# Gates of a seven-product set issued one and two jobs later, and the sets' weights asked for at the last low part of the tile they replace

## The chip, the cores and the metric

The kernel runs on one core of one Trainium2 chip. The metric is the device time of one execution in microseconds (us), taken as the median of several executions. A core has five engines that run beside each other: TensorE (PE, with PEld for its weight loads), VectorE (DVE), ScalarE (ACT), GpSimd (POOL), and SyncE (SP), which here only issues transfers (DMA).

## What is computed

One decoder block on 512 tokens of width 1024. The part that matters here is the projection of the normed input `u` by the wide matrix `w_in`, and the gates cut from it:

```python
u = rmsnorm(x, ln1_g[i])
proj = u @ w_in[i]
q, k, v, pool_in, z, xbc, dt_raw, gate_pre = jnp.split(proj, split_idx, axis=-1)
...
gates = jax.nn.sigmoid(gate_pre + b_gate[i]).reshape(b, s, N_BRANCH, D_MODEL)
merged = gates[:, :, 0] * y_a + gates[:, :, 1] * y_b + gates[:, :, 2] * y_c
x = x + merged @ w_o[i]
```

`y_b` is the pooled branch; its gate is the one that the change moves. After this comes a gated feed-forward block and a last norm.

## The kernel before

**Numbers in two parts.** Every matrix product is made from a high and a low part of each operand: `wh` is the weight rounded on ACT to TensorE's fast 32-bit form (`cast`, L186, the copies at L195), `wl` is what is left, a subtraction on DVE (`lows`, L208, at L215). A product is three matmuls, high by high, weight-high by activation-low, weight-low by activation-high, in that order (`mm3`, L228). So PE needs `wh` when a product starts, and `wl` for its last third.

**Jobs.** The work is a list of jobs, each one block of weights and a body of matmuls. Before the body of job n is written down, its `prepare` (L1785) writes the low part of job n+1, the cast of job n+2 and the fetch of job n+3. The cast's two halves are held back in a list, `second`, and written by `flush` within the body. There are two buffers for raw weights, three for `wh`, two for `wl`. A job can have a function `then` (L222), which is called right after its low part. Between jobs stand `Call`s, plain functions run at that place of the list. PE, ACT, DVE and POOL work in the order in which the program is written (L106, L1808), each through its own queue; SP's order is laid out by a scheduler from what a transfer has to wait for.

**Sets of seven.** Four times the kernel computes a 2x2 block product by seven products and not eight. The first of these gives values for attention (`v_pair`, L584); after it come three, set 0, 1 and 2 (`set_of_sevens`, L699; L1569 to 1572), on columns of q, of k and of gates. Set 0 makes gates 2 to 5 of branch 1; set 1 makes q and k alone; set 2 one q, one k, and gates 0 and 1. The seven jobs are called one to seven. In a set's job each product has two column blocks of twelve matmuls, 128 weight columns by 256 tokens (`body`, L760): four high by high, four with the activation's low part, four with the weight's low part, then the same for the second block; after each block `flush`, after both `use`, which reads the result from PSUM. Jobs of the values' seven come before, and the jobs of the three sets are interleaved by the list at L1581: one, five, two, three, six of set 0, one of set 1, seven of set 0, five of set 1, four of set 0, and so on.

**The quarter tiles.** One tile of 128x1024 numbers (a `w3`, from a pool of two) holds two quarters of a set's weights, `W[0]` and `W[1]`, each 128x4x256 numbers. `load` (L706) asks for them on SP. Then they are worked on in place: after the low part of one, `W[0] += W[1]` (DVE, L349) and the other quarters are added to `W[1]` by two accumulating transfers of POOL (L370); after the low parts of three and of six, `W[0]` takes in those jobs' raw weights (L349). Five reads the first sum, seven reads `W[1]`, four reads `W[0]` last. The values' seven use two such tiles of their own; its seven is the last reader of one of them and its four of the other, and these are the buffers that set 0 and set 1 take over. Set 2 takes over that of set 0, whose last reader is four of set 0. The calls that load set 0 and set 1 stand behind the bodies of the values' six and seven (L1578), that of set 2 stands before four of set 0 (L1585).

**Gates.** `gate_sink` (L1211) makes one gate of 128 columns by 512 tokens. A gate on the left side is ready in two halves: `two` adds on DVE (L1222) and takes the sigmoid of the first half on ACT (L1216), `four` takes the sigmoid of the second half from PSUM and multiplies the branch's result `MG` (tiles `yo`) by the gate on DVE (L1219). A gate on the right side: `put` subtracts on DVE (L1230), once with six and once with seven, and after the second time takes the sigmoid of the whole (L1216) and multiplies (L1219). Set 0 has two gates of either side, so its seven writes, on DVE, subtraction, multiplication, subtraction, multiplication, each multiplication behind a sigmoid on ACT.

**Sends.** The values' results `v` are sent by SP to tiles `vr` (L606), four small transfers for each block of tokens; they are read by the attention products at L841, long after the sets.

## Time and profile before

| | |
|---|---|
| Median of the runs | 1034.19 us (3 runs, 1032.52 to 1035.01) |
| The profiled execution: its own time | 1035.22 us |
| Its span, first to last instruction | 1033.4 us |
| Granted TensorE clock, mean | 0.997 |
| PE busy | 1022.2 us, 99% |
| PEld busy | 868.8 us, 84% |
| DVE busy | 698.8 us, 68% |
| ACT busy | 485.1 us, 47% |
| POOL busy | 161.2 us, 16% |
| Instructions | 13679 |
| Read from HBM | 118.48 MB, 117 GB/s over the span |
| The values' sevens start on PE | 206.6 us |
| The three sets run on PE | 235.8 to 311.6 us |

Times in the views are us from the start of the span. In a timeline a row has its start, its length, the engine, the line of the kernel, the operation, what it writes and reads, and how many instructions are merged in it; in square brackets stands how long its engine had been idle before it, and what ended that. Successive matmuls overlap, so the distance between the starts of two rows is the pace, and the length of a row is more than that. In a table by windows each row has the window, its length, the busy time of PE, PEld, DVE, ACT and POOL with their numbers of instructions, then the granted clock (1.00 is full speed), the busy share of the DMA engines and the GB/s that they moved. A row of a list of waits has who waited for whom, the us in total, how often, and the longest. The chain of waits is the work that ended last, followed back from the end, and shown in order of time.

### The profile page before, as it was taken

To read this page: it belongs to the slowest core of one execution; us is meant where nothing else is said; L and a number is where in the kernel's file an instruction comes from. 1 tells how busy PE (TensorE), PEld (TensorE's weight loads), DVE (VectorE), ACT (ScalarE), POOL (GpSimd) and SP (SyncE) were. 2 spreads that over 40 slices of the span, in tenths; PEclk is the share of its full clock that TensorE was granted. 3 is DMA by queue.
4 is the path that set the end of the run, shared out by engine and by line. 5 is a ranking of instruction groups with operands and counts; after the bars stand their busy time and mean duration, and the time that the engine had idled before them with its cause. 6 is when DMAs were issued, how large, how long until landed. Compare 5 with 4: busy or idle time off the path is not lost.

```text
span 1033.4 us, 13679 instructions
## 1 busy us (share of the span) xinstructions
PE 1022.2 (99%) x5420; PEld 868.8 (84%) x5420; DVE 698.8 (68%) x938; ACT 485.1 (47%) x811; POOL 161.2 (16%) x135
## 2 busy tenths in 40 slices
PE   9999999999999999999999999999999999999997
PEld 9998878899998888888888888898888888888885
DVE  5563566776767758766768656766768677666775
ACT  6432554455545564557445324545444443443342
POOL 1770000001100004210152501101111001111120
PEclk9999999999999999999999999999999999999999
DMA  8344312156453234552254525443223324323142
GB/s 289 115 127 139 102 62 75 31 116 170 103 133 123 82 109 116 143 133 68 68 152 147 179 82 203 168 144 121 82 100 124 103 82 162 122 82 123 62 143 82
DMA packets 121919, 123.16 MB, mean 119 GB/s; under 512 B 5603, under 2 KB 104230, under 8 KB 121855
## 3 DMA queue, kind: packets, MB, share of 16 engines
q1 hardware_dynamic: 118543, 119.07, 36.6%
q0 software_dynamic: 2720, 2.36, 1.7%
q8 instruction: 42, 0.69, 0.3%
q10 hardware_dynamic: 592, 0.86, 0.2%
q14 instruction: 22, 0.18, 0.1%
HBM read 118.48 MB, written 2.22 MB: 117 GB/s over the span
## 4 chain that ended last, share of the span: by engine, by line
PE 95%; DVE 2%; ACT 1%; DMA 1%; issue 0%; SPq 0%; ACTq 0%; DVEq 0%
PE pa L234 32%; PE pu L234 22%; PE p L234 14%; PE pb L234 8%; PE pqk L234 6%; PE pa L1696 2%; PE ps L800 1%; PE pu L1482 1%; PE ppw L234 1%; PE pt L828 1%; PE po L841 1%; PE py L1126 1%; DVE wl L215 1%; PE pa L1653 1%; DMA w<-in_w_in_dram 1%; PE pyo L1133 1%
## 5 line engine op out<-in xcount | busy, mean ns | idle before, releaser
L215 DVE TENSOR_TENSOR wl<-raw,wh 128x2048 fp32r<-128x2048 f32 (+3 forms) x94 | 208.7, 2222 | 44.9 <-ACT wh L195 35.6
L195 ACT CAST wh<-raw 128x1024 fp32r<-128x1024 f32 (+3 forms) x186 | 180.5, 994 | 46.8 <-DVE raw L339 26.3
L1343 DVE SCALAR_TENSOR_TENSOR hc<-pu,fcol,hc 128x510 f32<-128x510 f32 x88 | 65.8, 748 | 60.9 <-ACT hc L1340 59.3
L234 PE MATMUL pa<-uh,wh 128*128 128x512 f32 x336 | 86.5, 399 | 0.0
L234 PE MATMUL pu<-uh,wl 128*128 128x512 f32 (+1 forms) x352 | 83.7, 380 | 0.0
L234 PE MATMUL pu<-uh,wh 128*128 128x512 f32 (+1 forms) x352 | 83.5, 379 | 0.0
L234 PE MATMUL pu<-ul,wh 128*128 128x512 f32 (+1 forms) x352 | 83.5, 379 | 0.0
L234 PE MATMUL pa<-ul,wh 128*128 128x512 f32 x336 | 83.0, 389 | 0.0
L234 PE MATMUL pa<-uh,wl 128*128 128x512 f32 x336 | 83.0, 389 | 0.0
L234 PEld LDWEIGHTS pu<-uh,wl 128*128 128x128 f32 x352 | 64.1, 188 | 12.8 <-DVE wl L215 0.3
L234 PEld LDWEIGHTS pu<-ul,wh 128*128 128x128 f32 x352 | 64.2, 188 | 12.5
L234 PEld LDWEIGHTS pu<-uh,wh 128*128 128x128 f32 x352 | 64.1, 188 | 12.4
L234 PEld LDWEIGHTS pa<-ul,wh 128*128 128x128 f32 x336 | 63.1, 188 | 13.3
L234 PEld LDWEIGHTS pa<-uh,wl 128*128 128x128 f32 x336 | 63.1, 188 | 13.1
L1348 POOL TENSOR_TENSOR hc<-hc 128x512 f32<-128x512 f32 x22 | 30.4, 1383 | 278.9 <-DVE hc L1343 243.9
L234 PEld LDWEIGHTS pa<-uh,wh 128*128 128x128 f32 x336 | 61.2, 188 | 12.8 <-issue 0.7
L1340 ACT ACTIVATE hc<-pu,fcol,fcol 128x512 f32<-128x512 f32 x40 | 31.2, 779 | 80.3 <-PE pu L234 80.1
L195 ACT CAST wh<-w 128x512 fp32r<-128x512 f32 (+2 forms) x50 | 35.3, 748 | 21.6 <-DVE w L349 10.2
L821 ACT ACTIVATE sb<-sb,both 128x128 f32<-128x128 f32 (+1 forms) x72 | 30.0, 418 | 31.8 <-DVE both L818 21.7
L370 POOL DMA_DIRECT2D w<-in_w_in_dram x10 | 12.3, 1229 | 203.8 <-DVE w L349 150.8
L215 DVE TENSOR_TENSOR wl<-w,wh 128x1024 fp32r<-128x1024 f32 (+2 forms) x25 | 38.4, 1540 | 8.1 <-ACT wh L195 5.9
L1345 ACT ACTIVATE hc<-hc 128x512 f32<-128x512 f32 x22 | 13.9, 632 | 42.7 <-DVE hc L1343 42.7
(381 smaller groups left out, 1950.1 us busy)
## 6 DMA issues: line engine op xcount, KB each, us to landing
raw<-in_ffn_w_up_dram SPq DMA_DIRECT2D x22, 1024.0 KB
raw<-in_w_in_dram SPq DMA_DIRECT2D x21, 1024.0 KB
raw<-in_ffn_w_down_dram SPq DMA_DIRECT2D x11, 1024.0 KB
raw<-in_w_in_dram SPq DMA_DIRECT2D x20, 512.0 KB
raw<-in_w_o_dram SPq DMA_DIRECT2D x8, 1024.0 KB
raw<-in_w_b_dram SPq DMA_DIRECT2D x4, 1024.0 KB
al<-ad SPq DMA_DIRECT2D x16, 256.0 KB
w<-in_ffn_w_down_dram SPq DMA_DIRECT2D x4, 1024.0 KB
```

The lines of the kernel that those rows point to most:

```text
L195: act.copy(job.high[:, :, o], job.raw[:, :, o])
L215: (eng or dve).tensor_tensor(l[:, :, o], job.raw[:, :, o], h[:, :, o].bitcast(F32), OP.subtract)
L234: pe.matmul(ps, l, r, start=first and n == 0, stop=last and n == total - 1, skip_group_check=again)
L370: pool.dma_start(W[1][:, k:k + 2, at:at + n], src[:, k:k + 2, :], accum_op=OP.add)
L800: pe.matmul(pss[i][:, o:o + w * P], q[r, n * P:(n + 1) * P], k[r, kb * P:(kb + w) * P], start=True, stop=True)
L821: act.activation(sb[:, off:off + w * P], sb[:, off:off + w * P], AF.Exp, bias=nm[:, n, h:h + 1], accum_out=ls[:, n, h:h + 1])
L828: pe.transpose(pt[:, o:o + P], sb[:, o:o + P], eye)
L1340: act.activation(t, ps, AF.Identity, bias=ff["c1"][:, ff["b"] + m:ff["b"] + m + 1], scale=fw(2, m))
L1343: dve.scalar_tensor_tensor(t[:, sh:], ps[:, :S - sh], fw(k, m), t[:, sh:], OP.mult, OP.add)
L1345: act.activation(t, t, AF.Silu)
L1348: pool.tensor_tensor(a, a, t, OP.mult)
L1696: pe.matmul(first[2 * n + j][:, lo:hi], a[:, k, j * P:(j + 1) * P], b[:, k, lo:hi], start=a is wh and b is uh and k == 0, stop=a is wl and ...
```

## The change

A list `due` holds functions, and `settle` runs what it holds. It is called in each job of a set after the first column block's `flush`, and once after the last job of set 2. The gates put their sigmoids and multiplications there: the sigmoid of a left gate's first half runs within the next set job, the multiplication of a left gate too; a right gate's sigmoid runs in the next set job and its multiplication in the one after it. The sigmoid of a left gate's second half, which reads PSUM, stays where it was. The three loads become `then` of the jobs whose low part is the last reader of the tile that they replace: the values' seven (for set 0), the values' four (for set 1), four of set 0 (for set 2).

```diff
--- before.py
+++ after.py
@@ -694,7 +694,13 @@
     def turned_(ap):
         return ap.rearrange("p (j r) -> p r j", r=4)
 
-    ROLE, turn_of = {}, [0]
+    ROLE, turn_of, due = {}, [0], []
+
+    def settle():
+        todo = due[:]
+        due.clear()
+        for f in todo:
+            f()
 
     def set_of_sevens(lefts, rights, x, scales=(1.0, 1.0)):
 
@@ -767,6 +773,8 @@
                     lambda k: parts[k][0], lambda k: parts[k][1], range(4),
                     fresh and c == 0, True, again=not fresh or c == 1)
                 flush()
+                if c == 0:
+                    settle()
             use(name, ps)
             turn_of[0] += 1
             if turn_of[0] % 2 == 0:
@@ -1220,17 +1228,20 @@
 
         def two(ps, r):
             dve.tensor_tensor(t[:, LO], ps, r, OP.add)
-            gate(t[:, LO], t[:, LO])
+            due.append(lambda: gate(t[:, LO], t[:, LO]))
 
         def four(ps):
             gate(t[:, HI], ps)
-            times()
+            due.append(times)
+
+        def all_():
+            gate(t, t)
+            due.append(times)
 
         def put(hi, x, y):
             dve.tensor_tensor(t[:, (LO, HI)[hi]], x, y, OP.subtract)
             if hi:
-                gate(t, t)
-                times()
+                due.append(all_)
 
         return (two, four) if left else put
 
@@ -1573,20 +1584,17 @@
         yield Call(load)
         yield from BC(8, 10, 256)
         yield from gate_jobs(1, 6, 8)
-        for i, job in enumerate(pair):
-            yield job
-            if i in (4, 5):
-                yield Call(loads[i - 4])
+        pair[5].then, pair[6].then, s[0]["four"].then = loads
+        yield from pair
         spare = BC(10, 12, P)
         for i, n in ((0, "one"), (0, "five"), (0, "two"), (0, "three"), (0, "six"), (1, "one"),
                      (0, "seven"), (1, "five"), (0, "four"), (1, "three"), (1, "two"), (1, "six"),
                      (2, "one"), (1, "seven"), (2, "five"), (1, "four"), (2, "three"), (2, "two"),
                      (2, "six"), (2, "seven"), (2, "four")):
-            if (i, n) == (0, "four"):
-                yield Call(loads[2])
             if (i, n) in ((2, "seven"), (2, "four")):
                 yield next(spare)
             yield s[i][n]
+        yield Call(settle)
         yield Call(lambda: attend(1))
         yield from BC(0, 8, 256)
         yield Call(ssd_start)
```

Line numbers behind the first piece are 6 to 11 higher in the changed kernel: L1219 becomes L1227, L1216 L1224, L1222 L1230, L1230 L1242, L711 L717.

The first place is DVE's queue around four of set 0, before. `gr` are gates, `yo` the branch's results, `five` and `r7` products of set 0; `wl_2488` is the low part of set 0's four, `wl_2526` of set 1's three, `wl_2560` of set 1's two, and `w3_2196` set 1's quarter tile.

```order
L1230 TENSOR_TENSOR gr_2412<-five_2312,r7_2480 128x256
L1219 TENSOR_TENSOR yo_1530<-yo_1530,gr_2412 128x512
L1230 TENSOR_TENSOR gr_2413<-five_2312,r7_2480 128x256
L1219 TENSOR_TENSOR yo_1597<-yo_1597,gr_2413 128x512
L215 TENSOR_TENSOR wl_2488<-w3_2148,wh_2451 128x1024
L215 TENSOR_TENSOR wl_2526<-raw_2452,wh_2490 128x1024
L349 TENSOR_TENSOR w3_2196<-w3_2196,raw_2452 128x4x256
L1219 TENSOR_TENSOR yo_1363<-yo_1363,gr_2344 128x512
L1219 TENSOR_TENSOR yo_1434<-yo_1434,gr_2345 128x512
L215 TENSOR_TENSOR wl_2560<-raw_2491,wh_2529 128x1024
```

And in the changed kernel (`wl_2484` is four's, `wl_2524` three's, `wl_2558` two's):

```order
L1242 TENSOR_TENSOR gr_2412<-five_2312,r7_2480 128x256
L1242 TENSOR_TENSOR gr_2413<-five_2312,r7_2480 128x256
L215 TENSOR_TENSOR wl_2484<-w3_2102,wh_2451 128x1024
L215 TENSOR_TENSOR wl_2524<-raw_2452,wh_2491 128x1024
L349 TENSOR_TENSOR w3_2154<-w3_2154,raw_2452 128x4x256
L1227 TENSOR_TENSOR yo_1530<-yo_1530,gr_2412 128x512
L1227 TENSOR_TENSOR yo_1597<-yo_1597,gr_2413 128x512
L215 TENSOR_TENSOR wl_2558<-raw_2492,wh_2527 128x1024
L1227 TENSOR_TENSOR yo_1363<-yo_1363,gr_2344 128x512
L1227 TENSOR_TENSOR yo_1434<-yo_1434,gr_2345 128x512
```

Four's low part has moved ahead of both multiplications of the right gates, and these stand behind the low part of set 1's three and the sum after it; the multiplications of the left gates stand behind the low part of set 1's two.

The second place is ACT's queue at the same time, before. `wh_2490` is the high part of set 1's three, `wh_2529` of set 1's two, `r7` and `five` are copies of products.

```order
L731 ACTIVATE r7_2480<-p_2253 128x512
L1216 ACTIVATE gr_2412<-gr_2412,col_133 128x512
L1216 ACTIVATE gr_2413<-gr_2413,col_133 128x512
L195 COPY wh_2490<-raw_2452 128x4x128 x2
L731 ACTIVATE five_2519<-p_2254 128x512
L195 COPY wh_2529<-raw_2491 128x4x128 x2
L1216 ACTIVATE gr_2344<-p_2253,col_133 128x256
L1216 ACTIVATE gr_2345<-p_2253,col_133 128x256
```

And now:

```order
L737 ACTIVATE r7_2480<-p_2253 128x512
L195 COPY wh_2491<-raw_2452 128x4x128
L1224 ACTIVATE gr_2412<-gr_2412,col_133 128x512
L1224 ACTIVATE gr_2413<-gr_2413,col_133 128x512
L195 COPY wh_2491<-raw_2452 128x4x128
L737 ACTIVATE five_2522<-p_2254 128x512
L195 COPY wh_2527<-raw_2492 128x4x128 x2
L1224 ACTIVATE gr_2344<-p_2253,col_133 128x256
L1224 ACTIVATE gr_2345<-p_2253,col_133 128x256
```

The two whole sigmoids have moved between the two halves of the next cast; the half sigmoids from PSUM stand where they stood.

The third place is SP's queue while the values' seven end, before: `raw_2249` is the raw weights of set 0's three, `w3_2148` set 0's quarter tile, `v` and `vr` the values.

```order
L183 DMA raw_2249<-in_w_in_dram 128x4x256
L711 DMA w3_2148<-in_w_in_dram 128x4x256
L606 DMA vr2_2119<-v2_2115 32x384
L606 DMA vr2_2121<-v2_2115 32x384
L606 DMA vr2_2123<-v2_2115 32x384
L606 DMA vr2_2125<-v2_2115 32x384
L711 DMA w3_2148<-in_w_in_dram 128x4x256
L606 DMA vr2_2119<-v2_2139 32x384
```

Behind the second half of set 0's tile, twelve sends stand ahead of set 1's tile, `w3_2196`. Now (`w3_2102` is set 0's tile and `w3_2154` set 1's):

```order
L183 DMA raw_2249<-in_w_in_dram 128x4x256
L717 DMA w3_2102<-in_w_in_dram 128x4x256 x2
L606 DMA vr2_2122<-v2_2118 32x384
L606 DMA vr2_2124<-v2_2118 32x384
L606 DMA vr2_2126<-v2_2118 32x384
L606 DMA vr2_2128<-v2_2118 32x384
L606 DMA vr2_2122<-v2_2142 32x384
L606 DMA vr2_2124<-v2_2142 32x384
L606 DMA vr2_2126<-v2_2142 32x384
L606 DMA vr2_2128<-v2_2142 32x384
L717 DMA w3_2154<-in_w_in_dram 128x4x256 x2
```

Set 0's second half has moved ahead of four sends, and set 1's tile ahead of eight. The instructions of every engine are the same as before in kind and number.

## Prediction

> **What bounds the kernel now.** I read the page's summed chain first, then the waits of PE, then PE's own timeline where it waits, then the chain of waits across those places.

> ```profile
> PE 95%; DVE 2%; ACT 1%; DMA 1%; issue 0%; SPq 0%; ACTq 0%; DVEq 0%
> ```

> TensorE (PE) carries 95% of the chain that ended last, so only time in which PE stands or runs slowly can be won. The list of PE's waits in the stretch of the sets has one row:

> ```profile
> PE p L234 <- DVE wl L215: 2.3, 2, 1.7
> ```

> Twice PE waits for a low part `wl`, which DVE makes. PE's timeline around them (start, length, group of four matmuls) gives the price, larger than 2.3 us:

> ```profile
> 239.10 0.64 PE L234 MATMUL p<-sal,wh 128*128 128x256 f32 x4
> 240.31 0.74 PE L234 MATMUL p<-sah,wl 128*128 128x256 f32 x4 [0.57 <-DVE wl L215]
> 240.89 0.64 PE L234 MATMUL p<-sah,wh 128*128 128x256 f32 x4
> ...
> 254.33 0.64 PE L234 MATMUL p<-sbl,wh 128*128 128x256 f32 x4
> 254.87 0.75 PE L234 MATMUL p<-sbh,wl 128*128 128x256 f32 x4
> 255.45 0.64 PE L234 MATMUL p<-sbh,wh 128*128 128x256 f32 x4
> ...
> 260.24 0.64 PE L234 MATMUL p<-ul,wh 128*128 128x256 f32 x4
> 262.63 1.00 PE L234 MATMUL p<-uh,wl 128*128 128x256 f32 x4 [1.75 <-DVE wl L215]
> 263.42 1.05 PE L234 MATMUL p<-uh,wh 128*128 128x256 f32 x4
> ...
> 265.98 0.81 PE L234 MATMUL p<-sbh,wh 128*128 128x256 f32 x4
> 266.62 0.64 PE L234 MATMUL p<-sbl,wh 128*128 128x256 f32 x4
> ```

> Undisturbed, groups start 0.48 us apart (254.33 and 254.87 are the first pair that is not). A job has six, 2.88 us, and needs `wl` at the third, 0.96 us after its start. So: **A**, five of set 0: 240.31 - 239.10 - 0.48 = 0.73, and 0.10 in the next step (0.58): 0.83. **B**, seven of set 0: 0.06 + 0.10 = 0.16. **C**, four of set 0: 262.63 - 260.72 = 1.91. **D**, the pace after C: five steps from 262.63 to 266.62 take 3.99, not 2.40: 1.59. Together 4.49 us. D is a lower clock, as the windows say (column before the DMA share):

> ```profile
> 260.00:264.00 4.00, 2.25 (x15) 2.05 (x14) 3.25 (x4) 3.26 (x6) 0.00 (x0) 0.87 0.33 52
> 264.00:268.00 4.00, 4.00 (x27) 4.00 (x26) 2.12 (x4) 1.78 (x4) 0.00 (x0) 0.71 1.07 308
> ```

> The chain of waits names what was late (start, length, what):

> ```profile
> 225.74 1.75 DVE wl L215
> ...
> 230.41 6.04 DMA w<-in_w_in_dram
> ...
> 236.54 1.24 DVE w L349
> ...
> 237.86 1.15 ACT wh L195 x2
> ...
> 239.03 1.24 DVE wl L215
> ...
> 257.08 0.61 ACT r L731
> ...
> 257.71 0.44 DVE gr L1230
> ...
> 258.17 0.73 ACT gr L1216
> ...
> 258.93 0.69 DVE yo L1219
> 259.62 0.34 DVE gr L1230
> ...
> 259.99 0.73 ACT gr L1216
> ...
> 261.36 1.23 DVE wl L215
> ...
> 262.63 32.47 PE p L234 x256
> ```

> For A it is the second half of set 0's quarter tile, asked for at 230.41 and landed at 236.45. For C it is a ping-pong: DVE subtracts, waits for ACT's sigmoid, multiplies, and again, with four's `wl` queued behind in order. After 262.63 PE runs 32.47 us on end.

> **The change, part by part.** No arithmetic and no transfer is added.

> *C, gates one job later, products two.* DVE's queue becomes subtract, subtract, `wl` of four. From the rows: 257.71 + 0.44 + 0.44 = 258.59, and `wl` (1.23) ends at 259.82. PE wants it at 260.72: 0.90 to spare, so C goes (-1.91). What the sigmoids now delay is ACT's next cast, and the multiplications the next low parts. Two more rows for these:

> ```profile
> 263.63 1.22 DVE L349 TENSOR_TENSOR w<-w,raw 128x1024 f32<-128x1024 f32 x1
> 266.73 1.29 DVE L1219 TENSOR_TENSOR yo<-yo,gr 128x512 f32<-128x512 f32 x2 [1.89 <-ACT gr L1216]
> ```

> On ACT: copy until 257.69, first cast half (1.15 / 2 = 0.58) until 258.27, two sigmoids (0.73 each) until 259.73, second half until 260.3. DVE then: `wl` of set 1's three until 261.5 (wanted at 260.72 + 1.92 + 0.96 = 263.60), the sum (1.22) until 262.8, two multiplications (1.29) until 264.05, `wl` of two until 265.3 (wanted 266.48), two more multiplications until 266.6, `wl` of six until 267.8 (wanted 269.36). All in time; with this cover gone each would cost its lateness.

> *E, what is late next.* While PE stood in C and D, DVE caught up; now it does not. Following the same queue on this unshifted scale (sum 1.22, two q of set 1 as long as the two k below, `wl`, sum, two k, each time 1.23 for `wl`), `wl` of set 1's seven ends at 275.05, with PE wanting it at 260.72 + 5 x 2.88 = 275.12: 0.07 to spare. Today it has more:

> ```profile
> 275.61 1.17 DVE L689 TENSOR_TENSOR k<-p,r 128x256 f32<-128x256 f32 x2
> 276.69 1.22 DVE L215 TENSOR_TENSOR wl<-w,wh 128x1024 fp32r<-128x1024 f32 x1
> 277.66 0.64 PE L234 MATMUL p<-sbh,wh 128*128 128x256 f32 x4
> ```

> Today `wl` ends at 277.91, wanted at 278.62: 0.71. So E is 0 to +0.25; I take +0.10.

> *A, loads asked for earlier.* The tile is free when `wl` of the values' seven ends (225.74 + 1.75 = 227.49); its first half is issued then already, the second behind four sends:

> ```profile
> 227.51 0.37 SPq L711 DMA_DIRECT2D w<-in_w_in_dram  x1
> 233.53 1.14 ACT L195 CAST wh<-w 128x512 fp32r<-128x512 f32 x2 [1.25 <-DMA w<-in_w_in_dram]
> 234.71 1.23 DVE L215 TENSOR_TENSOR wl<-w,wh 128x1024 fp32r<-128x1024 f32 x1 [1.83 <-ACT wh L195]
> 239.78 1.24 SPq L711 DMA_DIRECT2D w<-in_w_in_dram  x2
> 228.00:232.00 4.00, 4.00 (x25) 4.00 (x24) 2.79 (x3) 2.27 (x5) 0.00 (x0) 1.00 0.95 288
> ```

> Now both are issued together, the second near 228.0. With the same 6.04 us it lands near 234.1; if the wires set it (the raw block before it and both halves, 0.52 MB each, at 288 GB/s from 228.0) near 233.5. Then the first half bounds: cast at 233.53, `wl` of one ends 235.94, sum, cast, `wl` of five (236.54 to 240.27 in the rows, 3.73) ends at 239.70, 0.12 after the wish of 239.58, plus 0.10 for restarting. A shrinks by 0.58 at least, by 0.83 if the first half lands 0.2 sooner; I take -0.70. The four sends that slip behind it, and all of `vr`, feed attention far behind these sets. Set 1's halves leave the queue after 8 sends, not 16; 16 took from 227.51 to 239.78, so near 234. No wait of PE's stood behind their first reader, so this alone wins nothing. Set 2's load had waited for `wl` of four anyway and follows it; its readers are not on the chain.

> *B.* Seven's `wl` was 0.02 us late because its cast, at the head of ACT's queue, began late:

> ```profile
> 251.26 1.14 ACT L195 CAST wh<-w 128x512 fp32r<-128x512 f32 x2 [2.33 <-PE p L234]
> ```

> Its buffer had come free with set 0's three, 3 us before, so I read the wait as one for POOL's accumulating loads into the same tile, which ran beside set 1's halves. Those now run earlier, and the sum that POOL waits for ends about 0.6 earlier: B goes (-0.16; bound 0).

> *D.* The slow stretch follows C alone; A's 0.73 left the next groups at 0.48. Without C I take D as gone (-1.59; bound 0).

> *Set 2's gates* slip behind three of the four casts of the next column block, one multiplication behind its `wl`; a later `wl` moves by about 0.7 us, and a block of 48 matmuls runs ahead of it, of which half is

> ```profile
> 311.78 5.46 PE pa L234 x24
> ```

> Sum: -0.70 - 0.16 - 1.91 - 1.59 + 0.10 = **-4.3 us**; bounds -4.49 and -0.58 - 1.91 + 0.25 = -2.2. Against the profiled execution's own 1035.22 (span 1033.4 and 1.8 around it) that is 1030.9, span 1029.1. That execution is 1.03 above the median of the runs, 1034.19, so for the median I forecast **1029.9**.

> **The rivals.** *The clock is not C's doing.* Then D stays, or it was not there in most of the timed runs: gain 2.7, 1031.5. For it: one occurrence is all the trace has. Against: no other slow stretch stands beside an unbroken PE. [...]

> *The earlier request wins nothing* (the second half still lands at 236.45 because the engines are full, 0.95 in 228 to 232): A stays, gain about 3.4, 1030.8. Against: in the wires' reckoning it lands at 233.5.

> *The first half is late.* Both halves now share the engines; if the first lands x later than 233.53, `wl` of one (it ends at 235.94, wanted at 239.58 - 2.88 = 236.70, so 0.76 to spare) waits x - 0.76 and five 0.88 more, with 0.10 for restarting; beyond x = 2.7 the first wait reaches C's length and brings D back: x + 0.22, 1.59 and E's 0.10 against 4.49 today. From x = 2.7 the kernel is no faster; at x = 6 it loses 3.4: 1037.6. For: it took 6.0 us as it is. Against: it is first in its queue, and x = 6 is twice that.

> **How the numbers follow.** Forecast 0.60, clock 0.20, no gain from the request 0.10, first half late 0.10 (half of it beyond 0.3%). 0.3%, 3.1 us, is about what a measurement of this kernel can tell from no change, so faster means under 1031.1. Of the forecast 0.53 lies there, of the clock rival 0.06, of the third 0.06: faster 0.65; slower 0.05; within 0.30. Range: bounds 1029.7 to 1032.0 from the median, and 0.8 to 1.4 for its scatter (the runs lie 1.7 below to 0.8 above theirs): 1028.3 to 1032.8. It leaves out most of the last rival.

> **What would show it.** Right: no PE wait for `wl` over 0.3 us between 235 and 310, steps of 0.48 throughout four and the job after it, clock 1.00 in every window there; second half issued before 229; DVE's two subtractions at L1242 back to back. Wrong: a slow stretch without a wait (D was not C's), a first half cast after 234.3, or a new wait at set 1's seven above 0.25. A gain seen here but missing at the end would mean that PE waits later for something I did not see.

## The result and the profile after

| | before | after |
|---|---|---|
| Median of the runs beside each other | 1034.20 us (8 runs, 1032.07 to 1035.01) | 1030.94 us (8 runs, 1029.93 to 1031.95) |
| Ratio, 95% interval | | 0.9972, 0.9961 to 0.9983 |
| Profiled execution: own time, span | 1035.22, 1033.4 us | 1029.93, 1028.2 us |
| Granted clock, mean | 0.997 | 0.999 |
| PE busy | 1022.2 us, 99% | 1019.2 us, 99% |
| The three sets on PE | 235.76 to 311.62: 75.86 us | 234.91 to 306.29: 71.38 us |

By the medians the kernel is 3.26 us faster (0.32%), by the ratio 0.28%, and the interval is clear of no change. The prediction drew its border of faster at 1031.1, and the median lies 0.16 below it. The forecast was 1029.9, the range 1028.3 to 1032.8.

The summed chain of after is PE alone, and the list of PE's waits (us in total, times, longest) has no row from the sets any more; its longest is at the start:

```profile
PE 98%; DVE 1%; ACT 0%; issue 0%; DVEq 0%; ACTq 0%
```

```profile
PE pa L1661 <- DVE relb L502: 1.1, 1, 1.1
```

PE's timeline of after at five of set 0 (where A was) and at four of set 0 (where C and D were):

```profile
238.25 0.64 PE L234 MATMUL p<-sal,wh 128*128 128x256 f32 x4
238.73 0.64 PE L234 MATMUL p<-sah,wl 128*128 128x256 f32 x4
...
258.41 0.64 PE L234 MATMUL p<-ul,wh 128*128 128x256 f32 x4
258.89 0.64 PE L234 MATMUL p<-uh,wl 128*128 128x256 f32 x4
259.37 0.64 PE L234 MATMUL p<-uh,wh 128*128 128x256 f32 x4
```

Every step is 0.48. In the table by windows, in the stretch where C and D were, PE and DVE are busy throughout and the granted clock is 1.00:

```profile
260.00:264.00 4.00, 4.00 (x36) 4.00 (x35) 4.00 (x6) 2.41 (x6) 0.00 (x0) 1.00 1.11 328
```

DVE's timeline of after shows how: both subtractions in one row, then four's low part, and the multiplications (L1227) behind the sum:

```profile
255.88 0.76 DVE L1242 TENSOR_TENSOR gr<-five,r 128x256 f32<-128x256 f32 x2 [2.23 <-ACT r L737]
256.56 1.22 DVE L215 TENSOR_TENSOR wl<-w,wh 128x1024 fp32r<-128x1024 f32 x1
258.22 1.23 DVE L215 TENSOR_TENSOR wl<-raw,wh 128x1024 fp32r<-128x1024 f32 x1 [0.44 <-ACT wh L195]
259.36 1.22 DVE L349 TENSOR_TENSOR w<-w,raw 128x1024 f32<-128x1024 f32 x1
260.50 1.29 DVE L1227 TENSOR_TENSOR yo<-yo,gr 128x512 f32<-128x512 f32 x2
```

Four's low part ends at 257.78 and PE wants it at 258.89.

So between these two profiles the sets give 75.86 - 71.38 = 4.48 us: A, B, C and D, whole. The other part of the 5.2 us between the spans is no work of the change. The first long row on PE, 38 warm-up matmuls, before and after:

```profile
1.06 7.29 PE L1653 MATMUL pa<-ones 128*128 128x128 f32 x38 [1.06 <-DVE relb L502]
```

```profile
1.06 6.42 PE L1661 MATMUL pa<-ones 128*128 128x128 f32 x38 [1.06 <-DVE relb L502]
```

The same row took 6.36 to 7.43 us in the profiles of the experiments below, and 6.36 to 7.29 in the two profiles of the kernel before. One pair of profiles thus shows more than the medians (5.2 against 3.26), and the experiments are there to tell which of the four gains come in every execution. The batches of runs stem from different chips, so each median is compared with the kernel before in its own batch.

### The profile page after: what moved, and what is told of

It reads as the page before. It is cut to its first block, busy times and chain, and to the rows that moved or that the text cites. A ratio compares the mean times of both kernels' runs of the same rounds, so it can differ in the third digit from the quotient of the medians.

```text
span 1028.2 us, 13683 instructions
## 1 busy us (share of the span) xinstructions
PE 1019.2 (99%) x5420; PEld 866.3 (84%) x5420; DVE 698.6 (68%) x938; ACT 485.1 (47%) x811; POOL 161.7 (16%) x135
## 4 chain that ended last, share of the span: by engine, by line
PE 98%; DVE 1%; ACT 0%; issue 0%; DVEq 0%; ACTq 0%
PE pa L234 32%; PE pu L234 22%; PE p L234 17%; PE pb L234 8%; PE pqk L234 6%; PE pa L1704 2%; PE ps L808 1%; PE pu L1493 1%; PE ppw L234 1%; PE pt L836 1%; PE po L849 1%; PE py L1134 1%; PE pa L1661 1%; PE pyo L1141 1%; PE pst L1120 0%; PE pxs L1088 0%
## 5 line engine op out<-in xcount | busy, mean ns | idle before, releaser
L215 DVE TENSOR_TENSOR wl<-raw,wh 128x2048 fp32r<-128x2048 f32 (+3 forms) x94 | 208.6, 2221 | 46.0 <-ACT wh L195 35.6
L195 ACT CAST wh<-raw 128x1024 fp32r<-128x1024 f32 (+3 forms) x186 | 180.8, 993 | 45.6 <-DVE raw L339 26.1
L234 PE MATMUL pa<-uh,wh 128*128 128x512 f32 x336 | 86.5, 399 | 0.0
L234 PE MATMUL pu<-uh,wl 128*128 128x512 f32 (+1 forms) x352 | 83.7, 380 | 0.0
L234 PE MATMUL pu<-uh,wh 128*128 128x512 f32 (+1 forms) x352 | 83.5, 379 | 0.0
L234 PE MATMUL pu<-ul,wh 128*128 128x512 f32 (+1 forms) x352 | 83.5, 379 | 0.0
L234 PE MATMUL pa<-ul,wh 128*128 128x512 f32 x336 | 83.0, 389 | 0.0
L234 PE MATMUL pa<-uh,wl 128*128 128x512 f32 x336 | 83.0, 389 | 0.0
L234 PEld LDWEIGHTS pu<-uh,wl 128*128 128x128 f32 x352 | 64.1, 188 | 12.8 <-DVE wl L215 0.3
L234 PEld LDWEIGHTS pu<-ul,wh 128*128 128x128 f32 x352 | 64.2, 188 | 12.5
L234 PEld LDWEIGHTS pu<-uh,wh 128*128 128x128 f32 x352 | 64.1, 188 | 12.4
L234 PEld LDWEIGHTS pa<-ul,wh 128*128 128x128 f32 x336 | 63.1, 188 | 13.3
L234 PEld LDWEIGHTS pa<-uh,wl 128*128 128x128 f32 x336 | 63.1, 188 | 13.1
L234 PEld LDWEIGHTS pa<-uh,wh 128*128 128x128 f32 x336 | 61.2, 188 | 12.8 <-issue 1.0
L195 ACT CAST wh<-w 128x512 fp32r<-128x512 f32 (+2 forms) x50 | 35.4, 748 | 17.7 <-DVE w L349 8.8
L215 DVE TENSOR_TENSOR wl<-w,wh 128x1024 fp32r<-128x1024 f32 (+2 forms) x25 | 38.5, 1540 | 6.5 <-ACT wh L195 4.4
```

Source lines behind the costliest of these rows:

```text
L195: act.copy(job.high[:, :, o], job.raw[:, :, o])
L215: (eng or dve).tensor_tensor(l[:, :, o], job.raw[:, :, o], h[:, :, o].bitcast(F32), OP.subtract)
L234: pe.matmul(ps, l, r, start=first and n == 0, stop=last and n == total - 1, skip_group_check=again)
```

## The experiments

### The loads alone

```diff
-                due.append(lambda: gate(t[:, LO], t[:, LO]))
+                gate(t[:, LO], t[:, LO])
-                due.append(times)
+                times()
-                due.append(all_)
+                gate(t, t)
+                times()
```

This is the changed kernel with the gates as they were.

> Loads as in the change, gates as before. Both theories: the wait at set 0's five (0.83 us) and the one at its seven (0.16) are gone, the wait of 1.9 us at its four stays, because DVE's queue there is as before. Theory 1 (the slow stretch follows that wait in every execution): the profile shows 1.6 us of slow pace behind it, and the time is 0.9 to 1.0 us under the kernel before. Theory 2 (it follows only in some executions): the same gain in the median, but the profile may show the 1.9 us wait with full pace behind it. Rival of the prediction (the earlier request wins nothing): the wait at five is still 0.8.

Measured: 1034.53 us, ratio 1.0008 (0.9999 to 1.0017); sets 75.60 us. PE's timeline (start, length, group) has all but B:

```profile
239.12 0.64 PE L234 MATMUL p<-sal,wh 128*128 128x256 f32 x4
240.22 0.74 PE L234 MATMUL p<-sah,wl 128*128 128x256 f32 x4 [0.46 <-DVE wl L215]
...
262.39 1.03 PE L234 MATMUL p<-uh,wl 128*128 128x256 f32 x4 [1.75 <-DVE wl L215]
263.22 1.05 PE L234 MATMUL p<-uh,wh 128*128 128x256 f32 x4
```

A is still 0.62 + 0.10, although both halves were asked for together, at 227.52. In this execution the early request wins little. What bounds A then is the first half: its cast starts at 234.02, 6.5 us after the issue (6.0 in the profile before, from 227.51 to 233.53):

```profile
234.02 1.14 ACT L195 CAST wh<-w 128x512 fp32r<-128x512 f32 x2 [1.73 <-DMA w<-in_w_in_dram]
```

### The gates alone

```diff
-        pair[5].then, pair[6].then, s[0]["four"].then = loads
-        yield from pair
+        for i, job in enumerate(pair):
+            yield job
+            if i in (4, 5):
+                yield Call(loads[i - 4])
...
+            if (i, n) == (0, "four"):
+                yield Call(loads[2])
```

> Gates as in the change, loads as before. The wait at set 0's four is gone with what follows it, those at five and seven stay (0.8 to 1.0 together). Theory 1: 3.4 to 3.5 us under the kernel before. Theory 2: 1.9 us and a part of the 1.6, so 2.0 to 3.0 in the median of the runs.

Measured: 1030.87 us, ratio 0.9974 (0.9964 to 0.9983), beside 1033.57 for the kernel before; sets 71.39 us. The whole gain is here. C and D are gone, and in this execution A and B too, with the loads where they were: the second half was asked for at 230.86, as late as before, and the first half, asked for at 227.96, was cast at 233.48, after 5.5 us.

### The multiplications alone

```diff
-            due.append(lambda: gate(t[:, LO], t[:, LO]))
+            gate(t[:, LO], t[:, LO])
...
-                due.append(all_)
+                gate(t, t)
+                due.append(lambda: due.append(times))
```

The sigmoids stand where they stood before; only the multiplications come later.

> Loads as in the change; the sigmoids stand where they stood before, only the multiplications are issued later. If it is DVE's queue alone that made four's low part late, as the prediction's sum has it, DVE's order is the changed one and the kernel is as fast as the changed one (3.3 us under before, 0.1% either way), with no wait of PE for a low part in the sets. If the sigmoids had to move too, a wait of 0.3 to 1.9 us stays at four of set 0 or the job after it.

Measured: 1031.07 us, ratio 0.9977 (0.9967 to 0.9986); sets 71.55 us, no C, no D, A 0.17. DVE's order is that of the change. ACT's is not, and it costs nothing: the ping-pong ended because DVE no longer waits between subtraction and low part.

### Set 1's load where it was

```diff
-        pair[5].then, pair[6].then, s[0]["four"].then = loads
-        yield from pair
+        pair[5].then, s[0]["four"].then = loads[0], loads[2]
+        for i, job in enumerate(pair):
+            yield job
+            if i == 5:
+                yield Call(loads[1])
```

> As the change, but set 1's tile is asked for where it was before. The wait at five of set 0 is gone. If the 0.16 us at seven came from the accumulating loads running beside set 1's halves, as the prediction read it, seven's cast begins 2 to 3 us after its buffer came free and a wait of 0.1 to 0.2 us is back there; if it came from the late sum alone, the cast begins within 0.5 us and there is none. The time is that of the changed kernel within 0.2 us either way.

Measured, one run: 1031.86 us; sets 72.26 us. Seven of set 0 ran at 0.48 throughout, so B did not come back, although set 1's halves were asked for late again (236.37 and 241.98, in the profile before 239.78 and 0.57 behind it). Against the expectation A stood at 0.82, with the first half cast 6.7 us after its issue, although both halves were asked for as in the change.

### The kernel before, again

No edit.

> The kernel before, unchanged, profiled and timed once more. In the first profile PE waited 1.91 us at set 0's four (C) and then ran 5 steps in 3.99 us instead of 2.40 (D, 1.59 us). Theory 1 (the half pace follows that wait in every execution): C of 1.8 to 2.0 us and behind it again about 1.6 us of slow steps, and all timed runs lie in one heap of about 1 us. Theory 2 (the half pace follows only in some executions): the runs fall into two heaps about 1.7 us apart, of about equal size, the later one at a mean granted clock of .996 to .997 and the earlier at .998 to .999; the profile may show C without D, and then its three sets take about 74 us and not 75.9.

Measured: 1032.82 us (10 runs), beside 1034.13 for 26 further runs of the same code on the same chip (ratio 0.9994, 0.9985 to 1.0003); sets 73.46 us. C is there, to the hundredth, and D is not:

```profile
258.81 0.64 PE L234 MATMUL p<-ul,wh 128*128 128x256 f32 x4
261.20 0.74 PE L234 MATMUL p<-uh,wl 128*128 128x256 f32 x4 [1.75 <-DVE wl L215]
261.78 0.64 PE L234 MATMUL p<-uh,wh 128*128 128x256 f32 x4
```

The same 1.75 us of standing, the same line, and the clock stays at 1.00 (its windows are shown further down). A (0.07) and B (0) are not there either. The runs that stood beside the experiments say how often D comes. By the mean granted clock of each run they fall into two heaps, with a few runs between:

| the kernel before, beside | clock .998 or .999: runs, mean span | clock .996 or .997: runs, mean span | median |
|---|---|---|---|
| the first four experiments | 13, 1031.13 us | 11, 1032.87 us | 1033.57 us |
| this one and the next three | 5, 1030.92 us | 21, 1032.37 us | 1034.13 us |
| the raw block moved, and the twenty chains of standing times | 3, 1031.00 us | 9, 1032.29 us | 1033.93 us |
| the last pair | 14, 1030.74 us | 6, 1032.43 us | 1032.72 us |

The heaps are 1.3 to 1.7 us apart, about D's 1.59. In all, 47 of 82 runs lie in the slower one. The mean clock is a rough sign of D: one run at .997 has a span of only 1030.2 us, and three at .998 or .999 have 1031.7 to 1031.9. The changed kernel has 1 of 29 there.

### The change, again

No edit.

> The changed kernel, unchanged, profiled and timed once more beside the others. Theory 2 with a request that wins nothing: 2.7 to 3.3 us under the kernel before (ratio .9969 to .9974), all runs in one heap at a clock of .998 to .999; in the profile no wait at set 0's four, and a wait at set 0's five of 0 to 0.9 us by when the first half of set 0's quarter tile has landed: none below 5.3 us after its issue, 0.8 at 6.7. Theory of the prediction (the request for the second half wins 0.7): no wait at set 0's five whenever the first half lands up to 6 us after its issue.

Measured: 1031.28 us, ratio 0.9972 (0.9963 to 0.9982); sets 72.38 us. This time A is there. SP's queue, ACT and PE:

```profile
226.14 0.54 SPq L183 DMA_DIRECT2D raw<-in_w_in_dram  x1
227.42 0.93 SPq L717 DMA_DIRECT2D w<-in_w_in_dram  x2
```

```profile
234.21 1.14 ACT L195 CAST wh<-w 128x512 fp32r<-128x512 f32 x2 [2.01 <-DMA w<-in_w_in_dram]
```

```profile
239.21 0.64 PE L234 MATMUL p<-sal,wh 128*128 128x256 f32 x4
240.41 0.74 PE L234 MATMUL p<-sah,wl 128*128 128x256 f32 x4 [0.57 <-DVE wl L215]
```

The first half needed 6.8 us. In the first profile of the changed kernel no cast waited for it: ACT's copy ended and the cast began at 231.32, at most 4.7 us after the issue at 226.65.

### Five one job later

```diff
-        for i, n in ((0, "one"), (0, "five"), (0, "two"), (0, "three"), (0, "six"), (1, "one"),
+        for i, n in ((0, "one"), (0, "two"), (0, "five"), (0, "three"), (0, "six"), (1, "one"),
```

> The changed kernel with set 0's five one job later (one, two, five, three, six in place of one, five, two, three, six). Five is the first reader of the sum in the quarter tile; its low part then has 2.88 us more before PE wants it, and two reads raw weights, not the tile. If the first half's landing sets what is left of the wait at set 0's five, this wait is 0 in every execution, even with a landing 7 us after the issue, and the kernel takes 0.2 to 0.5 us less than the changed one (the mean of waits of 0 to 0.8 us). If five's wait stems from something else (DVE or ACT too full), it moves one job on and the time stays within 0.2 us. If the sums and results that are now used in another order make something late behind, it shows as a new wait at three or six and the time is up to 1 us longer.

Measured: 1034.85 us, ratio 1.0012 (1.0003 to 1.0020): all of the gain is lost, against the first expectation. Five does not wait any more, although the first half needed 7.1 us (one itself, its first reader, waits 0.24 for it). But three now waits, and far longer than the third expectation had it. ACT and PE:

```profile
245.14 0.62 ACT L195 CAST wh<-w 128x512 fp32r<-128x512 f32 x1 [4.35 <-DVE w L349]
245.66 0.90 ACT L1224 ACTIVATE gr<-gr,col 128x256 f32<-128x256 f32 x2
246.47 0.60 ACT L195 CAST wh<-w 128x512 fp32r<-128x512 f32 x1
246.98 0.58 ACT L737 ACTIVATE five<-p 128x512 f32<-128x512 f32 x1
```

```profile
244.13 0.64 PE L234 MATMUL p<-sah,wl 128*128 128x256 f32 x4
247.61 0.74 PE L234 MATMUL p<-sbh,wh 128*128 128x256 f32 x4 [2.84 <-ACT five L737]
...
248.66 1.02 PE L234 MATMUL p<-sbh,wl 128*128 128x256 f32 x4
249.48 1.05 PE L234 MATMUL p<-sbh,wh 128*128 128x256 f32 x4
```

Five and three write the same PSUM bank (`role`), and five's copy out of it now stands on ACT behind the cast of a later job, the sigmoids, and that cast's second half. The cast waits for the sum that follows three's low part. This costs 3.00 us of waiting and four steps at 0.82 to 0.86 instead of 0.48. Here the half pace begins only with the third group, 1.05 us after the wait's end. Ten of its 11 runs show a clock of .996 or .997.

### Standing times of two kinds

In the feed-forward's up stage PE transposes a constant, other engines copy it `n` times, and PE transposes the last copy before the last third of a product. Ten such chains with POOL's copies in the first kernel, twenty with ACT's in the second. This adds work that the reference does not have; the output is the same.

```diff
+                g = MM("gap")
+                pe.transpose(g[:, :P], eye, eye)
+                act.copy(gap_a, g[:, :P])
+                t, u = gap_a, gap_b
+                for _ in range(n):
+                    pool.tensor_copy(u, t)
+                    t, u = u, t
+                pe.transpose(g[:, P:2 * P], t, eye)
```

> The changed kernel with ten chains put into the feed-forward's up stage: in ten of its jobs PE transposes a constant, ACT copies it, POOL copies it 0, 1, 2, 3, 4, 2, 3, 4, 6 and 3 times, and PE transposes the last copy before it goes on; this makes PE stand for ten stretches of about 0.6 to 4 us, apart by some 12 us of unbroken matmuls. Theory 1 (a fixed length decides): behind every stretch above one length, below 1.9 us, matmuls run at half pace for 2 to 4 us, behind none below it, and equal stretches always do the same. Theory 2 (it depends on where the stretch falls in windows that run freely): stretches of equal length, about 1.5 to 3 us, are sometimes followed by half pace and sometimes not; those under about 1.5 never, those over about 4 always. A third (the half pace at set 0's four had nothing to do with standing): no half pace behind any of the ten. The kernel is 15 to 40 us longer.

Measured: 1087.23 us, the longer for it. A group of eight matmuls normally lasts 1.98 us, with 1.81 to the next start. After 0.59 us of standing the first lasts 2.09, with its restart; after 2.84 it lasts 3.53:

```profile
710.70 0.33 PE L1493 MATMUL gap<-eye,gap_a 128*128 128x128 f32 x1 [0.59 <-ACT gap_a L1488]
710.78 2.09 PE L1495 MATMUL pu<-uh,wl 128*128 128x512 f32 x8
...
735.77 0.47 PE L1493 MATMUL gap<-eye,gap_b 128*128 128x128 f32 x1 [2.84 <-POOL gap_b L1491]
735.89 3.53 PE L1495 MATMUL pu<-uh,wl 128*128 128x512 f32 x8
```

All nine waits of 2.84 to 4.67 us are followed by the slow group, so the third theory falls; POOL gave no length between 0.59 and 2.84, which left the first two open. Hence the second kernel, with `act.copy` in place of `pool.tensor_copy` and `n` from 3 to 7.

> The changed kernel with twenty chains in the feed-forward's up stage: PE transposes a constant, ACT copies it 4 to 8 times in a row (0.26 us each), and PE transposes the last copy before it goes on; PE stands some 1.3 to 2.3 us each time, with over 10 us of unbroken matmuls between. The run before showed no half pace behind a wait of 0.59 us and half pace behind each of nine waits of 2.84 to 4.67 us. Theory 1 (a fixed length decides): one length between 1.3 and 2.3 parts those without from those with half pace, with no overlap. Theory 2 (where the wait falls in a window that runs freely): around 1.9 us waits of the same length stand in both groups, about half with and half without, with a share that grows with the length.

Measured: none of the seven waits of 1.40 to 2.01 us is followed by a slow group, each of the four of 2.67 and more is. Between them it goes either way: 2.06 no, yes, no; 2.18 yes, yes; 2.33 yes, yes; 2.39 no, no. Two of equal length, and a longer one without a slow group:

```profile
782.37 0.33 PE L1493 MATMUL gap<-eye,gap_b 128*128 128x128 f32 x1 [2.06 <-ACT gap_b L1491]
782.46 2.07 PE L1495 MATMUL pu<-uh,wl 128*128 128x512 f32 x8
...
858.96 0.33 PE L1493 MATMUL gap<-eye,gap_b 128*128 128x128 f32 x1 [2.06 <-ACT gap_b L1491]
859.05 3.30 PE L1495 MATMUL pu<-uh,wl 128*128 128x512 f32 x8
...
967.07 0.33 PE L1493 MATMUL gap<-eye,gap_a 128*128 128x128 f32 x1 [2.39 <-ACT gap_a L1491]
967.15 2.09 PE L1495 MATMUL pu<-uh,wl 128*128 128x512 f32 x8
```

No one length parts the two groups, so theory 1 falls.

What decides can be read from the granted clock. Each slow stretch in mid kernel lasts 3.41 us (two in the first of these kernels 6.83), and in one execution the stretches begin whole multiples of that length apart: in the second kernel at 767.42, 801.55 and 859.58, that is 34.13 and 58.03 us apart, 10 and 17 times 3.413. In the first profile of the kernel before, the slow stretch at 262.93 and the last fall of the clock, at 1030.93, are 768.00 us apart, 225 lengths. So in these executions the beginnings mark a grid of windows that runs through the whole. These are windows of that grid at the first two waits of 2.06 us (behind the length PE's busy time, before the DMA share the clock):

```profile
777.66:781.07 3.41, 2.65 (x13) 1.91 (x11) 3.37 (x4) 1.58 (x5) 1.59 (x1) 1.00 0.00 0
781.08:784.49 3.41, 2.12 (x10) 1.79 (x11) 2.71 (x3) 1.15 (x4) 0.00 (x0) 1.00 0.00 0
784.49:787.90 3.41, 3.41 (x17) 2.83 (x16) 1.50 (x2) 1.67 (x3) 0.00 (x0) 1.00 0.89 278
...
856.17:859.58 3.41, 1.35 (x7) 0.87 (x6) 3.03 (x4) 1.76 (x6) 0.00 (x0) 1.00 0.60 232
859.58:862.99 3.41, 3.41 (x9) 2.64 (x8) 0.00 (x0) 0.60 (x1) 0.00 (x0) 0.50 0.00 0
```

The first wait is split over two windows, 0.76 and 1.29 us, and the clock stays; the second lies in one, and the window behind it is granted half. The 2.39 us at 967.07 are split too, 0.71 and 1.68. In both kernels all 18 windows at full clock in which PE stands for 2.01 us or more are followed by a slow one, and none of the 16 in which it stands for 1.00 to 1.94.

The same grid explains D. The kernel before at its four of set 0, in the first profile and in the second:

```profile
259.52:262.93 3.41, 1.67 (x14) 1.46 (x13) 2.62 (x5) 2.94 (x6) 0.00 (x0) 1.00 0.43 66
262.93:266.34 3.41, 3.41 (x18) 3.41 (x17) 1.91 (x2) 0.45 (x2) 0.00 (x0) 0.50 0.76 209
```

```profile
257.55:260.96 3.41, 1.90 (x16) 1.69 (x15) 2.62 (x4) 2.40 (x5) 0.00 (x0) 1.00 0.51 67
260.96:264.37 3.41, 3.17 (x26) 3.18 (x27) 2.90 (x4) 1.82 (x5) 0.00 (x0) 1.00 0.59 166
```

(The second profile has no slow stretch there; its grid is counted back from 1025.55, where its clock falls at the end, by 225 lengths.) C's 1.75 us lie in one window in the first profile, and in that of the loads alone; in the second they are split into 1.51 and 0.24. If C falls anywhere in the grid, it lies whole in one window in (3.41 - 1.75) / 3.41 = 49% of the executions, and at most 63% if a little over 1.51 us is enough: an estimate from these figures. The runs have 47 of 82, 57%, but from batch to batch 30 to 81%, so the places are not evenly spread in each. Why the border lies between 1.51 and 1.75 us of a window in the sets, and between 1.94 and 2.01 in the up stage, was not found.

### The raw block behind the quarter tile

```diff
+        def first():
+            loads[0]()
+            fetch(s[0]["two"])
+            three = s[0]["three"]
+            raw = three.raw = wraw.tile([P, three.k, three.c], F32, name="raw", tag="raw")
+            dve.memset(raw[:, 0, 0:1], 0.0)
...
+                sp.dma_start(raw[:, :, at:at + n], src)
...
-        pair[5].then, pair[6].then, s[0]["four"].then = loads
+        pair[5].then, pair[6].then, s[0]["four"].then = first, loads[1], loads[2]
```

The one-column memset on DVE holds the block back until the tile's two halves are asked for; the rest is the change.

> The changed kernel with one transfer moved: the raw block of set 0's three (0.52 MB), which leaves SP's queue 1.3 us ahead of both halves of set 0's quarter tile, now leaves right behind them; nothing reads it before 240. Theory 1 (set 0's first half lands late because it shares the DMA engines with that block): the cast that waits for it starts at most 5.3 us after its issue (6.7 with the block ahead, in the last profile of the changed kernel), the wait at set 0's five is gone in every execution, and the median is 0.3 to 0.8 us under the changed kernel's, some 3.3 to 4 us under the kernel before. Theory 2 (the landing varies by itself): the first half is as late as before, and the time is that of the changed kernel within 0.2 us. If the block then comes too late for set 0's three, a new wait stands at three, of up to 1 us.

Measured: 1030.81 us, ratio 0.9970 (0.9960 to 0.9981), 3.12 us under the kernel before in place of theory 1's 3.3 to 4; sets 71.39 us, no wait of PE's in them. SP's queue and ACT's next cast:

```profile
227.65 0.93 SPq L717 DMA_DIRECT2D w<-in_w_in_dram  x2
228.67 0.45 SPq L1596 DMA_DIRECT2D raw<-in_w_in_dram  x1
```

```profile
232.31 1.14 ACT L195 CAST wh<-w 128x512 fp32r<-128x512 f32 x2
```

No idle time stands before this cast: the half was there at most 4.7 us after its issue. The median alone does not tell the two apart, so both ran once more, side by side:

> The changed kernel again, beside the one with the raw block of set 0's three moved behind, on the same chip. In three profiles so far its wait at set 0's five was 0 (the first) and 0.8 us (the second); theory 1 expects single runs from 1029.9 to 1031.9, spread over 2 us by that wait.

> The changed kernel with the raw block of set 0's three behind the quarter tile's halves, once more, beside the changed kernel on the same chip. Theory 1 (the block ahead is what makes the first half late in part of the executions): no wait at set 0's five in the profile, the cast of the first half at most 5.3 us after its issue, and runs whose upper end is 0.5 to 0.8 us lower, the median 0.2 to 0.5 lower. Theory 2 (the landing varies by itself): the median within 0.2 us of the changed kernel's, with the same upper end.

Measured: the change 1031.10 us (11 runs, 1030.20 to 1031.81), ratio 0.9980 (0.9971 to 0.9989), sets 72.39 us, A 0.82 again, first half after 6.8 us; the block moved 1030.65 us (10 runs, 1030.38 to 1030.93), ratio 0.9976 (0.9966 to 0.9985), sets 71.39 us, first half after at most 4.7 us. The means of the runs differ by 0.37 us (1031.01 less 1030.64; 95% interval from the runs' scatter about 0.0 to 0.75), together with the earlier runs of both kernels by 0.39 (0.13 to 0.65). The upper end fell by 0.9. A is set by the first half's landing, and the block ahead of it delays that in most executions; this version takes less time than both kernels, by little.

## Why the prediction came out as it did

**C (-1.91): right.** The wait is the same 1.91 in every profile with the old order on DVE (before twice, the loads alone) and in none with the new. Its reason, the multiplications between subtraction and low part, is shown by the kernel that moves them alone. Four's low part was to have 0.90 us to spare; it has 1.11.

**D (-1.59): right in size, wrong as a certainty.** The prediction said "the slow stretch follows C alone" from one occurrence (its 1.91 us of standing are 1.75 and the restart). It follows C in the first profile and in that of the loads alone, and does not in the second of before: C causes it when its 1.75 us fall into one window of the clock's grid, and not when they are split. By the clocks it stands in 47 of 82 runs. The rival "in most of the timed runs not there" is thus half true. A median takes whichever heap holds the middle: the change's gain was 3.3 us beside the runs whose median run had D (1034.20), and 1.6 us beside the last, in which 14 of 20 had none (1032.72 to 1031.10). So it is partly luck, of the runs that the median was taken from, that the gain came as near to the forecast 4.3 as it did.

**A (-0.70): the step that failed.** "Now both are issued together, the second near 228.0" holds (SP issued both within 0.93 us), and "then the first half bounds" too. What fails is "cast at 233.53": the prediction kept the first half's landing while giving it company. With both together and the raw block ahead, the cast came 5.9 to 7.1 us after the issue in eight of nine profiles (the two with chains included) and 4.7 or less in one, against 5.5 to 6.0 in three with the halves apart. So A is still 0.4 to 0.8 in six of the eight profiles that ask for both halves together and keep the order of the jobs and the block, 0.17 in a seventh, and 0 in the eighth, which is the first one taken. That one meets every sign that the prediction named; in the other two of the same kernel PE waits 0.57 us at five, above the 0.3 it allowed. On the median the loads win nothing: 1030.87 without them (ratio 0.9974), 1030.94 to 1031.28 with them (0.9972 to 0.9980). That the kernel with the loads alone was as slow as 1034.53 is explained by A and D in part only: its four runs at a clock of .998 or .999 have spans of 1031.9 to 1032.8 us, on average 1.3 above the kernel before's at that clock, of which A's 0.72 can be about half; the rest stays open. The third rival named this mechanism; its x was at most 1.1, far from the 2.7 at which the change would have won nothing.

**B (-0.16): gone, but not shown to be the change's.** It is missing in the second profile of before as well, and in the kernel that leaves set 1's load late. The reading by POOL's accumulating loads is not confirmed; 0.16 us that comes and goes was not followed further.

**E (+0.10): measured 0.** PE reached the last third of set 1's seven at 273.29; its low part is the first in this row of DVE's timeline of after, and so ready by 272.6:

```profile
271.37 2.44 DVE L215 TENSOR_TENSOR wl<-w,wh 128x1024 fp32r<-128x1024 f32 x2
```

0.7 us to spare, not 0.07. Of the 0.63 between, 0.21 is four's low part, which ended that much earlier against PE than forecast, and 0.42 is a shorter queue behind it. That queue was added up from whole lengths, while DVE's rows overlap: 258.22, 259.36 and 260.50 above start 1.14 apart, with lengths of 1.23 and 1.22.

**The sum.** Where the median run has D, C + D = 3.50 remains of the forecast 4.3; 3.26 was measured. A's 0.70 is most of what is missing, and B's 0.16 is not shown to be won; the rest is less than the interval of the ratio can tell, about 1.1 us either way. The reference was loose too: the whole 4.3 was carried from one profiled execution over to the median, without asking which of its terms the median run had.

## What to carry to other kernels

An instruction that waits for another engine belongs behind the work that the bounding engine wants next, even if it is ready first (C, 1.91 us here); and before reordering jobs, look at what each engine's queue holds back in order, results waiting to leave PSUM above all (2.84 us of standing in the kernel with five later). Asking earlier for the quarter tile won nothing on the median (1030.87 us without, 1030.94 to 1031.28 with); moving the large transfer that stood ahead of it to behind it won a little, 0.39 us in the mean: delay what has time, rather than ask earlier. Take a second profile of the kernel before: a term seen once may be in half of the runs (D, by the clocks, in 47 of 82), and a median can count it whole or not at all.
